# Gradient along rows of an 8192 x 8192 array: from groups of three loads and three stores to strict turns, with a late first store

## The chip, the cores and the metric

One core of one Trainium2 chip. The metric is the device time of one execution in microseconds (us); lower is better. Times are medians of several executions. A ratio is the mean time of one kernel's fast runs over that of the other's fast runs of the same rounds, so it is not quite the ratio of the medians that stand beside it.

Three words are used throughout. A **transfer** is one load or one store of a set, 8.39 MB, that 16 DMA engines carry together; each engine moves 8 rows of 64 KB, one packet per row. A **mark** is the completion write of one engine at the end of its part of a transfer, so a transfer has 16 of them; the **spread** is the time from the first to the last of the 16. A **turn** is the point at which an engine goes from the last packet of a load to the first packet of a store. Packets and marks are records in the trace. They don't name the engine; I put each packet behind the one whose end it follows.

## The reference

```python
def setup_inputs():
    return {"x": np.random.randn(8192, 8192).astype(np.float32)}

def reference(x):
    return np.gradient(x, axis=1)
```

Inside a row, an element of the result is half the difference of its two neighbours; at both ends of a row it is the plain difference of the first or last two elements. 268 MB are read and 268 MB written.

## The kernel before

A set is 256 rows, two per partition (64 KB per partition). There are 32 sets and three slots in SBUF. A set is loaded to a slot, VectorE computes it in place, shifted by 64 elements, and the slot is stored. All loads and stores are issued by SyncE on one queue. `chain` names the steps that an instruction has to wait for, in place of the scheduler's own finding.

```python
    R = 2; NB = 3; SH = 64; W = R * m
    slots = [pool.tile([P, SH + W], f32, ...) for k in range(NB)]
    ...
    def load(i):
        b = slots[i % NB]
        ins = nc.sync.dma_start(out=b[:, SH : SH + W], in_=x_sets[i])
        loads.append(chain(i, ins, *([stores[i - NB]] if i >= NB else [])))

    with tc.manual_schedule():
        for i in range(NB):
            load(i)
        for i in range(nsets):
            ...  # ends: GpSimd takes the 4 edge differences of the set
            for r in range(0, R, nr):        # one pass; two in the last set
                ...  # halved: VectorE, 0.5 * (right - left), whole set
                ...  # placed: VectorE or GpSimd copies the edges in
                ins = nc.sync.dma_start(
                    out=out_sets[i, :, r * m : (r + nr) * m], in_=b[:, r * m : (r + nr) * m]
                )
                stores[i] = chain(i, ins, placed)
                at = [halved]
            if i % NB == NB - 1:
                for k in range(i + 1, min(i + 1 + NB, nsets)):
                    load(k)
```

So the queue holds three loads, three stores, three loads and so on: eleven turns in all.

## Time and profile before

| | before |
|---|---|
| median of 3 runs | 1247.24 us (1247.1 to 1248.14) |
| span of the profiled run | 1245.0 us |
| one queue, share of 16 engines' span | 99.8% |
| VectorE busy | 554.8 us (45%) |
| one transfer, mark to mark | 19.32 us |

The prediction below shows the lines that this table rests on. One more view carries the argument: the table of DMA issues of the page, with the time from issue to landing (us) at the end of each line.

```profile
out_dram<-slot SPq DMA_DIRECT2D x2, 4096.0 KB, 20.2
slot<-in_x_dram SPq DMA_DIRECT2D x32, 58.0
out_dram<-slot SPq DMA_DIRECT2D x31, 40.3
```

A transfer takes 19.3 us, but a load lands 58.0 us after its issue and a store 40.3: two transfers, and one, lie ahead of it in the queue. A queue this full does not run dry before the end of the run, and until then a wait of the issuing engine costs nothing.

### The profile page before, as it was taken

What the parts mean: (1) busy time and instruction counts of PE and PEld (TensorE: products, weight loads), DVE (VectorE), ACT (ScalarE), POOL (GpSimd) and SP (SyncE); (2) the same over time, 40 slices, a digit from 0 to 9 for tenths busy, and PEclk for the clock granted to TensorE, in tenths of its full rate; (3) what the DMA queues carried; (4) which work ended last, traced back from release to release, by engine and by line L of the source; (5) the groups of instructions that cost most, each with busy time, mean ns of one, the idle gap of its engine ahead of it and who ended that gap; (6) DMA issues with size and microseconds to landing.
All of it is one profiled execution on the core that took longest, in us unless ns stands there. A gap on an engine that the chain in (4) does not pass through costs nothing.

```text
span 1245.0 us, 241 instructions
## 1 busy us (share of the span) xinstructions
DVE 554.8 (45%) x54; POOL 8.8 (1%) x48
## 2 busy tenths in 40 slices
DVE  2850483079009603850582079009603840591083
POOL 0000000000000000000000000000000000000000
DMA  9999999999999999999999999999999999999999
GB/s 404 438 436 419 425 438 438 438 438 438 434 427 421 436 438 438 436 438 432 432 419 438 436 438 432 436 434 432 423 436 436 436 438 436 430 427 430 436 411 404
DMA packets 9361, 536.88 MB, mean 431 GB/s; under 512 B 1040, under 2 KB 1040, under 8 KB 1040
## 3 DMA queue, kind: packets, MB, share of 16 engines
q1 hardware_dynamic: 9360, 536.88, 99.8%
q14 instruction: 1, 0.01, 0.0%
HBM read 268.44 MB, written 268.44 MB: 431 GB/s over the span
## 4 chain that ended last, share of the span: by engine, by line
another core or an unknown queue 74%; DVE 18%; DMA 3%; issue 2%; POOL 1%; SPq 0%; POOLq 0%
DVE slot L81 18%; DMA slot<-in_x_dram 3%; POOL ends L70 0%; POOL slot L92 0%; SPq L60 0%; DVE slot L92 0%; POOLq L127 0%
## 5 line engine op out<-in xcount | busy, mean ns | idle before, releaser
L81 DVE CUSTOM_DVE_ANT_0 slot<-slot 128x16382 f32<-128x16382 f32 (+1 forms) x33 | 551.3, 16706 | 667.9 <-POOL ends L70 667.9
L70 POOL TENSOR_TENSOR ends<-slot 128x4 f32<-128x4 f32 x32 | 6.3, 198 | 988.8 <-DMA slot<-in_x_dram 988.8
L92 DVE COPY slot<-ends 128x4 f32<-128x4 f32 (+1 forms) x21 | 3.6, 172 | 0.7
L92 POOL COPY slot<-ends 128x4 f32<-128x4 f32 x12 | 2.3, 190 | 207.9 <-DVE slot L81 207.9
L116 POOL MEMSET const-bfloat16-1.0<- 128x1 bf16 x1 | 0.1, 102 | 0.0
L116 POOL MEMSET const-uint8-127<- 128x1 uint8 x1 | 0.1, 102 | 0.0
L116 POOL MEMSET const-float32-0.0<- 128x1 f32 x1 | 0.1, 99 | 0.2 <-issue 0.2
L116 POOL MEMSET const-float32-1.0<- 128x1 f32 x1 | 0.1, 99 | 0.0
## 6 DMA issues: line engine op xcount, KB each, us to landing
out_dram<-slot SPq DMA_DIRECT2D x2, 4096.0 KB, 20.2
slot<-in_x_dram SPq DMA_DIRECT2D x32, 58.0
out_dram<-slot SPq DMA_DIRECT2D x31, 40.3
```

Source lines behind the costliest of these rows:

```text
L70: ins = nc.gpsimd.tensor_sub(out=ends[:, i, :, :], in0=xin[:, :, 1 : m : m - 2], in1=xin[:, :, 0 : m - 1 : m - 2],)
L81: ins = nc.vector._custom_dve(dve_ops.TENSOR_TENSOR_REDUCE_SUB_MAX, out=b[:, c0:c1], in0=b[:, SH + c0 + 1 : SH + c1 + 1], in1=b[:, SH + c0 ...
L92: ins = placer.tensor_copy(out=res[:, :, 0 : m : m - 1], in_=ends[:, i, r : r + nr, :])
L116: nc = _bacc.Bacc("TRN2", target_bir_lowering=False, num_devices=1)
```

## The change

Two things at once. After the first three loads and two stores, a load follows each store, so the direction changes after every transfer (30 turns; the recorded texts below say 31). And the first store is no longer issued while the loads run: an otherwise useless matmul, which itself waits for the second set's edges, is set ahead of it, so that the third load has run out of the engines before the store arrives. The intent is to start the stores on all 16 engines at once.

```diff
+    unread = psum.tile([1, 128], f32, name="unread", tag="unread")
...
                 placed = chain(i, ins, halved)
-                ins = nc.sync.dma_start(out=out_sets[i, ...], in_=b[...])
-                stores[i] = chain(i, ins, placed)
+                if i == 0:
+                    at = [halved]
+                    first = placed
+                    continue
+                if i == 1:
+                    pause = nc.tensor.matmul(
+                        out=unread[:], lhsT=slots[0][:, 0:1], rhs=slots[0][:, 0:128], start=True, stop=True
+                    )
+                    follow(pause, placed, "towards the end of the third load")
+                    follow(store(0, 0, R, first), pause, "after the third load")
+                store(i, r, nr, placed)
                 at = [halved]
-            if i % NB == NB - 1:
-                for k in range(i + 1, min(i + 1 + NB, nsets)):
-                    load(k)
+            if 1 <= i and i + 2 < nsets:
+                load(i + 2)
```

(`follow` adds one wait between two instructions, and `store` issues the same transfer as before.)

More of the change, by code (lines that the diff above doesn't have):

```diff
@@ L4 @@
 import concourse.tile as tile
-from concourse import bass_utils, dve_ops
+from concourse import bass_utils, dve_ops, mybir
 from concourse._compat import with_exitstack
@@ L41 @@
     ends = pool.tile([P, nsets, R, 2], f32, name="ends", tag="ends")
+    psum = ctx.enter_context(tc.tile_pool(name="psum", bufs=1, space=bass.MemoryType.PSUM))
+    unread = psum.tile([1, 128], f32, name="unread", tag="unread")
     loads, stores = [], [None] * nsets
@@ L56, in chain, with follow @@
         return ins
+    def follow(ins, needed, reason):
+        edge = mybir.DependencyInfo(mybir.DependencyClass.Sync, mybir.DependencyReason.DATA)
+        tc.add_manual_dep(ins.ins, needed.ins.name, edge, reason=reason)
     def load(i):
@@ L61, in load, with store @@
         loads.append(chain(i, ins, *([stores[i - NB]] if i >= NB else [])))
+    def store(i, r, nr, *needed):
+        ins = nc.sync.dma_start(
+            out=out_sets[i, :, r * m : (r + nr) * m], in_=slots[i % NB][:, r * m : (r + nr) * m]
+        )
+        stores[i] = chain(i, ins, *needed)
+        return ins
     with tc.manual_schedule():
@@ L93 @@
                 placed = chain(i, ins, halved)
-                ins = nc.sync.dma_start(
-                    out=out_sets[i, :, r * m : (r + nr) * m], in_=b[:, r * m : (r + nr) * m]
-                )
-                stores[i] = chain(i, ins, placed)
+                if i == 0:
[5 more added lines that the diff above has]
+                        out=unread[:], lhsT=slots[0][:, 0:1], rhs=slots[0][:, 0:128], start=True, stop=True
+                    )
+                    follow(pause, placed, "towards the end of the third load")
+                    follow(store(0, 0, R, first), pause, "after the third load")
+                store(i, r, nr, placed)
                 at = [halved]
-            if i % NB == NB - 1:
-                for k in range(i + 1, min(i + 1 + NB, nsets)):
-                    load(k)
+            if 1 <= i and i + 2 < nsets:
+                load(i + 2)
 _INS = ['x']
```

## The prediction

> **What bounds the kernel now.** I read the page's head and its slices first, then the DMA queue, then the issue-to-landing table, then the waits of the DMA queue and the timeline of the start and of the end; last I took the DMA packet records and the completion marks out of the trace.
>
> ```profile
> span 1245.0 us, 241 instructions
> DVE 554.8 (45%) x54; POOL 8.8 (1%) x48
> ...
> DMA  9999999999999999999999999999999999999999
> GB/s 404 438 436 419 425 438 438 438 438 438 434 427 421 436 438 438 436 438 432 432 419 438 436 438 432 436 434 432 423 436 436 436 438 436 430 427 430 436 411 404
> ...
> q1 hardware_dynamic: 9360, 536.88, 99.8%
> ```
>
> The reader is to see that VectorE is busy 45% of the span, while the DMA row holds a 9 in every one of its 40 slices and the one queue fills 99.8% of sixteen engines' span. The work is 536.88 MB each run, loads and stores together, and no edit of the order changes that. So the kernel is bound by the DMA engines, and only time in which an engine is idle or slower than its best can be won.
>
> How much is that? In the trace one packet is one partition's row of a set, 65,536 bytes; the minimum, the median and the 75th percentile of its duration are all 2.418 us. Sixteen engines each carry 8 such packets per transfer of 8.39 MB. From the completion marks one transfer follows another every 19.32 us nearly all the way through, in groups of loads and in groups of stores alike: 8.39 MB / 19.32 us = 434 GB/s. There are 32 loads and 32 stores (the last store in two halves), so 64 x 19.32 = 1236.5 us of the 1245.0 is transfer at the full rate. The other 8.5 us are:
> - 1.75 us before the first packet and 1.25 us after the last (first packet 1.75, last packet's end 1243.74);
> - about 0.6 us of slow first packets (some 3.0 us against 2.418);
> - about 0.8 us in the last store's two halves (9.72 us each by the mean of the engines, against 9.66) and in marks between transfers, with rounding;
> - 1.1 us at the first store: the third load's mark comes 20.47 us after the second's instead of 19.32, all 16 engines alike, as the last packet of that load takes 3.2 to 3.5 us;
> - the rest, some 3 us, on the slowest engines only, over the middle of the run. The engines' marks of one transfer lie 0.48 us apart at 62 us and 2.57 us apart from 876 us on. I found nearly all of it in one place: the last packet of the third load of a group, just before the engine turns to stores. At ten such turns after the first the last engine to finish lost, by my differences of the marks, about 0.0 to 0.2 us (seven turns) and 0.6 to 0.8 us (three turns, near 525, 642 and 759 us). At the turns from stores to loads I found nothing of note.
>
> The second view is the start and the end:
>
> ```profile
> 0.74 1.33 SPq L60 DMA_DIRECT2D slot<-in_x_dram  x3
> 22.70 0.20 POOL L70 TENSOR_TENSOR ends<-slot 128x4 f32<-128x4 f32 x1 [22.26 <-DMA slot<-in_x_dram]
> 22.93 17.22 DVE L81 CUSTOM_DVE_ANT_0 slot<-slot 128x16382 f32<-128x16382 f32 x1 [22.93 <-POOL ends L70]
> 40.19 0.17 DVE L92 COPY slot<-ends 128x4 f32<-128x4 f32 x1
> 40.39 40.08 SPq L94 DMA_DIRECT2D out_dram<-slot  x3
> ...
> 59.56 0.19 POOL L92 COPY slot<-ends 128x4 f32<-128x4 f32 x1 [17.32 <-DVE slot L81]
> 62.45 0.20 POOL L70 TENSOR_TENSOR ends<-slot 128x4 f32<-128x4 f32 x1 [2.71 <-DMA slot<-in_x_dram]
> ```
>
> Here the first store is issued at 40.39 us, in the middle of the load phase, and stands in the queue until the third load is through, at about 61.7 us. The copy on GpSimd at 59.56 ends at 59.75; it is the event that the new matmul waits for. And the rule of the buffers: the DMA queue's own waits are large but harmless, since a transfer is already under way behind each of them.
>
> ```profile
> SPq L94 <- DVE slot L92: 525.7, 21, 55.9
> SPq L60 <- DMA out_dram<-slot: 373.2, 29, 19.2
> ```
>
> **What the Trainium skill says.** "DMA: Bandwidth & Descriptors", section "Where 436 GB/s comes from", gives 435.2 GB/s for the 16 ports and says that the ports are the bottleneck; the 434 GB/s of a step above agrees, so I allow no gain in the rate itself. Its section "Queues, rings and completion order" says that each engine consumes descriptors in ring order and that nothing is FIFO across engines; the marks that drift from 0.48 to 2.57 us apart agree. "HBM Reference", section "Access", gives about 425 GB/s for a core streaming alone; the trace is a little above. For the added matmul, "TensorE: Matmul & The Clock Gate", section "Single matmul latency", has (219 + N)/1.2 ns cold for bf16, so 0.29 us for N = 128; no matmul is in the trace before, and this one is in float32, so I allow 0.3 to 0.7 us, an estimate.
>
> **The change part by part.**
>
> *Order.* From three loads, three stores to L0 L1 L2 S0 S1 L3 S2 L4 S3 L5 and so on to S29 L31 S30 S31. The same 65 transfers; the packets do not change. Does the new order starve the queue? Count in steps T of 19.32 us from the start of S0: S0 fills 0-1, S1 1-2, L3 2-3, S2 3-4, L4 4-5, S3 5-6, L5 6-7. L3 waits for S0's landing (at 1T plus some 1.5 us) and is wanted at 2T. S3 needs L3 landed (3T + 1.6 us), then 0.23 us of GpSimd, 17.22 us of VectorE and 0.2 us for the ends, so about 4T; it is wanted at 5T. L5 waits for S2, landed just after 4T, and sits behind S3 in the issuing engine, so about 4T + 2 us; it is wanted at 6T. Every later pair repeats this, and each transfer is issued about one T, 19 us, ahead. I expect no starving: **0 us**.
>
> *First store.* It leaves the third load alone. That load should then end 1.0 to 1.1 us earlier, near 60.7 (21.92 + 2 x 19.34 by the marks' mean). But the store now waits for 59.75 (copy) + 0.1 + 0.3 to 0.7 (matmul) + 0.1, so it is issued at about 60.5, and its first packet moves some 1.0 us after issue (the first load: issued 0.74, first packet 1.75), so 61.5; a start from idle costs the first packets up to 0.6 us, as at the start of the kernel. S0 then ends by its mean mark at about 81.0 to 81.6, against 81.07 before: **0 to +0.5 us**.
>
> *What the idle start buys.* All engines start the store together. The kernel's last store, where most engines had run dry, shows a spread of only 0.25 us. If it keeps the engines in step, the 3.2 us that the slowest engine loses between 62 and 1205 us can go: **0 to -3.2 us**.
>
> *The turns.* Load to store turns grow from 11 to 31 or so. If each cost what those ten cost on average, 0.31 us on the slowest engine, that would be 31 x 0.31 = 9.6 us in place of 3.1: **up to +6.5 us**. I don't believe the whole of it: once the engines were 2.57 us apart, more than a packet, the loss all but stopped, and in the new order no store is issued while a load is on its last packet (S3 comes at about 4T, at the end of a store), which before it always was.
>
> *End.* L31 lands, S30 has long been computed, so it follows at once; before, it was issued at 1203.88 and the early engines idled for over a microsecond. The end goes by the late engines, so this is worth **0 to -0.5 us**.
>
> *Sum.* With no loss at the turns: S0's mark at 81.4, + 59 x 19.32 + 2 x 9.72 = 1240.7, + 0.3 to the slowest engine + 1.25 after it = a span of 1242.3; the median time was 2.2 us over the span, so **1244.5 us**. With the losses as before it is about 1247.5, with 0.31 us at each turn about 1253.
>
> **The rivals.** First, *nothing gained*: the drift of the engines comes back at the more numerous turns and saturates near a packet's length, as before; the time is 1247 to 1248. The three costly turns out of eleven, without a visible rule, speak for it; against it, that the group turns coincided with issues. Second, *a turn penalty*: every turn costs, reads and writes of HBM now mix all the time; 1250 to 1254. For it: the loss sits at load to store turns alone. Against: at the turns near 178 and 1106 us there was next to none, and before, too, early engines stored while late ones loaded, with steps still of 19.32. Third, *a wait takes over*, where the compute of a set lies on the path since the loads are no longer a group ahead: each set late by 1 us would cost 30 us. The count of T above speaks against it, as VectorE needs 17.4 us in each 38.6.
>
> **How the range follows.** I give 45% to nearly no loss (1244 to 1245.5), 35% to a loss as before (1246 to 1248.5), 20% to more. The point is 1245.8, the range 1243.7 to 1251. 2% is 25 us: far more than all the idle there is (8.5 us), so faster by over 2% is all but excluded, and slower needs the third rival.
>
> **What would show it.** In the profile after: 99% or more of sixteen engines' span on the one queue and 9s in all slices (no starving); steps of 19.32 us between marks; the third load landing near 61 and the first store issued near 60.5 us; the marks' spread under 0.5 us for long (gain kept) or growing to over 2 us (first rival). GB/s under 430 in the middle slices would speak for the second, a wait of VectorE or of a store that ends with idle engines for the third. A step other than 19.32 us would make the prediction wrong.

## The result, and the profile after

The changed kernel took 1251.85 us in the median (1250.09 to 1253.26, 4 runs) against 1247.42 (1247.1 to 1248.14, 4 runs): 4.4 us more. The ratio is 1.0034, with an interval of 1.0017 to 1.0051. That is within 2%, as forecast, but the time lies outside the range.

The page of the changed kernel, its head, the slices and the queue:

```profile
span 1251.1 us, 246 instructions
...
DMA  9999999999999999999999999999999999999997
GB/s 402 436 436 402 436 436 436 432 436 434 425 436 432 436 436 430 417 427 436 436 434 436 427 434 432 434 436 436 436 436 436 434 430 434 436 427 434 425 436 339
...
q1 hardware_dynamic: 9360, 536.88, 99.5%
```

The engines are nearly as full as before (99.5% against 99.8%), and the DMA row shows no starved stretch before the last slice. Two slices are to be looked at. The fourth (some 94 to 125 us) moved 402 GB/s, where its neighbours have 436. And the last has a 7 and 339 GB/s, where before it had a 9 and 404: in the last 31 us some engines have finished and others have not.

The start of its timeline (start, duration, instruction, and in brackets the idle time before it with what ended it):

```profile
59.48 0.19 POOL L105 COPY slot<-ends 128x4 f32<-128x4 f32 x1 [17.32 <-DVE slot L94]
59.73 0.09 PEld L115 LDWEIGHTS unread<-slot 128*1 128x1 f32 x2 [59.73 <-POOL slot L105]
59.73 0.58 PE L115 MATMUL unread<-slot 128*1 128x128 f32 x2 [59.73 <-POOL slot L105]
60.34 0.83 SPq L70 DMA_DIRECT2D out_dram<-slot  x2
61.31 0.20 POOL L83 TENSOR_TENSOR ends<-slot 128x4 f32<-128x4 f32 x1 [1.63 <-DMA slot<-in_x_dram]
...
121.87 0.20 POOL L83 TENSOR_TENSOR ends<-slot 128x4 f32<-128x4 f32 x1 [60.36 <-DMA slot<-in_x_dram]
```

The pause works as meant: the matmul ends at 60.31, the store is issued at 60.34, and the third load is seen landed at 61.31, where before it was 62.45. The fourth load is seen landed at 121.87. Three transfers of 19.32 us lie between (two stores and the load itself), so 61.31 + 57.96 = 119.27 would do; 2.6 us are gone by then.

The waits of the DMA queue's issuer show that nothing new blocks it. Each column is: total us, times, longest.

```profile
SPq L70 <- DVE slot L105: 665.3, 19, 37.7
SPq L66 <- DMA out_dram<-slot: 71.1, 29, 20.0
SPq L70 <- PE unread L115: 58.3, 1, 58.3
```

The waits for stores to land are now short in total (71.1 us against 373.2 before), since a load is asked for later; the table of issues still has 58.5 us from a load's issue to its landing and 40.2 us for a store, as before. The queue stayed one to two transfers ahead, as the prediction counted.

The marks say where the 6.1 us between the two spans went. (The profiled run of the changed kernel was the slowest of its four, so its trace shows 6.1 us where the medians differ by 4.4.)

| from the marks, us | before | after | difference |
|---|---|---|---|
| first store done, mean of 16 engines | 81.07 | 80.65 | -0.42 |
| the next transfer takes (a store in both) | 19.32 | 20.10 | +0.78 |
| the one after it (a store; now the load of set 3) | 19.32 | 20.44 | +1.12 |
| sixth transfer done, last engine | 120.03 | 121.50 | +1.47 |
| from there to the 63rd transfer, last engine | 1104.34 | 1108.92 | +4.58 |
| spread of the 62nd transfer's marks | 2.57 | 8.02 | |
| last store, to the end | 19.37 | 19.37 | 0 |

The rows that add up are the fourth, the fifth and the last: 1.47 + 4.58 = 6.05 us, the difference between the last packets' ends (1243.74 and 1249.79). There are two losses, then. **One comes once, in the first 125 us, to all engines**: the first store is done 0.4 us sooner, and the next two transfers lose 1.9 us. **The other grows through the run and on the slow engines alone**: 57 transfers at 19.32 us are 1101.24; the last mark fell 3.1 us behind that before and 7.7 us after, while the first mark fell only 0.3 us behind after.

In both traces nearly all of the second loss sits in one packet of eight: the last packet of a load that is followed by a store. Summed over all loads of the changed kernel and averaged over the engines, the excess over 2.418 us of the eight packets of a load is 0.86, 0.00, 0.00, 0.00, 0.00, 0.03, 0.05 and 3.94 us; the first is the start of the kernel, the last the turns (0.9 of the 3.94 belongs to the load of set 3, so to the first loss).

### The profile page after: what moved, and what is told of

It is laid out like the page before. It is cut to its first block, busy times and chain, and to the rows that moved or that the text cites. A ratio compares the mean times of both kernels' runs of the same rounds, so it can differ in the third digit from the quotient of the medians.

```text
span 1251.1 us, 246 instructions
## 1 busy us (share of the span) xinstructions
PE 0.6 (0%) x2; PEld 0.1 (0%) x2; DVE 554.8 (44%) x54; POOL 8.9 (1%) x48
## 3 DMA queue, kind: packets, MB, share of 16 engines
q1 hardware_dynamic: 9360, 536.88, 99.5%
## 4 chain that ended last, share of the span: by engine, by line
another core or an unknown queue 68%; DVE 18%; DMA 8%; issue 3%; POOL 1%; PE 0%; SPq 0%; POOLq 0%
DVE slot L94 18%; DMA slot<-in_x_dram 7%; DMA out_dram<-slot 2%; POOL ends L83 0%; POOL slot L105 0%; PE unread L115 0%; SPq L66 0%; DVE slot L105 0%; POOLq L149 0%
## 6 DMA issues: line engine op xcount, KB each, us to landing
slot<-in_x_dram SPq DMA_DIRECT2D x32, 58.5
out_dram<-slot SPq DMA_DIRECT2D x31, 40.2
```

## The experiments

Two theories to begin with. **A**: the number of turns makes the drift, and the late first store is harmless. **B**: the late first store leaves the engines in a worse state for the whole run, and the turns are harmless. In the first four runs each part of the change was done alone.

**The changed kernel again (e0_after)**, without an edit, as the control.

> The changed kernel again, unaltered, as the control for the three runs beside it. Both theories: 1250 to 1253 us, 3 to 6 us over the kernel before, and a spread of the engines' completion marks that grows to 5 us or more.

Measured: 1251.65 us against 1248.23 on that chip, ratio 1.0036 (1.0023 to 1.005); the spread grew to 5.3 us. The result repeats.

**Strict turns alone (e1_alt_nopause).**

```diff
-                if i == 0: ...            # the deferred first store
-                if i == 1: ...            # the matmul and the two waits
                 store(i, r, nr, placed)
```

> Strict turns, but the first store issued as early as before (no matmul, no pause). Theory A (the number of turns from load to store makes the loss): 1250 to 1253 us as in the changed kernel, with the engines drifting apart by 5 us or more, and the 1.0 us loss at the first store back. Theory B (the late first store sets a bad state for the whole run): 1246 to 1248 us, spread under 3 us.

Measured: 1250.09 us (1248.08 to 1253.06), ratio 1.0016 (1.0003 to 1.0029), 2 us over the kernel before. The 1.0 us at the first store is back; the spread grew to 6.05 us, and the last engine lost 5.8 us from the sixth transfer to the 63rd. The drift belongs to the turns, but the turns alone give half of the loss in time. Its page shows the same end as the changed kernel's (a 7, and 344 GB/s), with no 402 in the fourth slice:

```profile
DMA  9999999999999999999999999999999999999997
GB/s 403 437 437 424 429 424 437 433 433 435 433 431 437 435 426 424 433 433 435 437 437 435 435 426 435 437 433 424 437 437 437 435 435 435 429 435 435 437 437 344
```

**The late first store alone (e2_grp_pause).**

```diff
-            if 1 <= i and i + 2 < nsets:
-                load(i + 2)
+            if i % NB == NB - 1:
+                for k in range(i + 1, min(i + 1 + NB, nsets)):
+                    load(k)
```

> Groups of three as before, but with the late first store. Theory A: 1246 to 1248 us, spread 2 to 3 us at the end, as before. Theory B: 1250 us or more, spread over 5 us. Besides, where the 1.0 us loss of the third load only waits for the first non-idle turn, about 1 us must come back at the next change of direction.

Measured: 1249.75 us, ratio 1.0013 (1.0001 to 1.0026), 1.5 us over the kernel before. Theory A missed here (the spread was 3.75 us in the end), and theory B too; the remark at the end of the expectation came true. By the marks, the third load lost nothing (before: 1.1 us), but the engines then stood idle, and the first store was done at 80.95 us in the mean, hardly sooner than before (81.07). Then the third store, ahead of the first load, lost 0.76 us, and the third load of the next group, at the first turn without a pause, 1.16 us in the mean of the engines. The timeline shows the latter:

```profile
159.93 0.20 POOL L83 TENSOR_TENSOR ends<-slot 128x4 f32<-128x4 f32 x1 [1.64 <-DMA slot<-in_x_dram]
...
180.31 0.20 POOL L83 TENSOR_TENSOR ends<-slot 128x4 f32<-128x4 f32 x1 [20.18 <-DMA slot<-in_x_dram]
```

The two loads are seen landed 20.38 us apart. In the kernel before, the same pair stood 19.36 us apart:

```profile
159.18 0.20 POOL L70 TENSOR_TENSOR ends<-slot 128x4 f32<-128x4 f32 x1 [1.64 <-DMA slot<-in_x_dram]
...
178.54 0.20 POOL L70 TENSOR_TENSOR ends<-slot 128x4 f32<-128x4 f32 x1 [19.16 <-DMA slot<-in_x_dram]
```

**Groups of two (e3_pairs)**, first store early.

```diff
-            if 1 <= i and i + 2 < nsets:
-                load(i + 2)
+            if i % 2 == 1:
+                for k in range(i + 2, min(i + 4, nsets)):
+                    load(k)
```

> Turns of two stores and two loads, first store early: 16 turns from load to store against 11 before and 31 in strict turns. Theory A: between the two, 1247.5 to 1250 us, spread 3 to 6 us. Theory B: as the kernel before, 1247 to 1248 us, since the first store is early.

Measured: 1250.01 us, ratio 1.0016 (1.0003 to 1.0028), spread 3.25 us. Theory B missed. The spread is in theory A's range, but it tells nothing, since three traces of groups of three ended with 2.6 to 3.9 us. What the last engine lost from the sixth transfer to the 63rd tells more: 5.3 us, against 3.1 and 4.2 in the two traces of the kernel before and 5.0 to 8.0 in the four of strict turns. Neither this nor the time tells 16 turns from 30.

So neither theory was whole. The two parts roughly add: 0.13% for the pause and 0.16% for the turns, against 0.36% for both on the same chip. The next run asks what the pause does. **C**: after an idle start of all engines, the next two changes of direction cost again, wherever in the run. **D**: such losses belong to the start of the run.

**The pause in the middle (e4_grp_gap_mid)**: groups of three, first store early, and the same matmul ahead of the store of set 15.

```diff
-                if i == 0:
+                if i == 15:
...
-                if i == 1:
+                if i == 16:
...
-                    follow(store(0, 0, R, first), pause, "after the third load")
+                    follow(store(15, 0, R, first), pause, "after the third load")
```

> Groups of three, first store early as before; the same pause, but ahead of the store of set 15, in the middle of the run. Theory C (an idle start of the engines costs again at the next two changes of direction, wherever it is): the transfer after the pause comes about 1 us late, the last store of that group before the next load loses 0.7 us and the next turn from load to store about 1.1 us on all engines; 1.5 us over the kernel before. Theory D (those losses belong to the start of the run, to addresses or queues used for the first time): no uniform loss of over 0.3 us at the next store to load turn, and 0.3 to 1 us over the kernel before.

Measured: 1250.14 us against 1247.78, ratio 1.0018 (1.0006 to 1.0031). The load of set 17 lost nothing at its turn; the store after the pause was done 2.33 us late in the mean (the early engines had stood idle until the store came, behind the late ones: the spread fell from 2.6 to 0.16 us); the last store of that group lost 0.74 us, and the load of set 20, at the next turn, 1.19 us on all engines. The time, 2.4 us over the kernel before, is more than the 1.5 us that theory C had, and clear of the 0.3 to 1 us of theory D. The timeline:

```profile
642.99 0.58 PE L115 MATMUL unread<-slot 128*1 128x128 f32 x2 [642.99 <-POOL slot L105]
643.61 18.98 SPq L70 DMA_DIRECT2D out_dram<-slot  x3
...
742.92 0.20 POOL L83 TENSOR_TENSOR ends<-slot 128x4 f32<-128x4 f32 x1 [1.64 <-DMA slot<-in_x_dram]
...
763.25 0.20 POOL L83 TENSOR_TENSOR ends<-slot 128x4 f32<-128x4 f32 x1 [20.13 <-DMA slot<-in_x_dram]
```

Again 20.33 us between two loads of a group, at the same distance from the pause as in the run with the pause at the start, but 583 us later. **Theory C holds**: the late first store takes away no cost. It trades the 1.0 to 1.1 us of the first turn for an idle gap of nearly the same size (0.8 to 1.0 us at the start of the run), and the first turn without a gap still pays its 1 us, later; the change from stores to loads ahead of it pays 0.7 to 0.8 us, which it does not without the pause (0.00 to 0.03 us at each such change in the trace of the kernel before). The kernel's own start is an idle start too, and after it the first turn pays 1.0 to 1.1 us, but the change back to loads nothing.

**Stores on ScalarE's queue (e5_two_queues)**, from the version with strict turns and no pause, to ask whether an engine pays for each change of direction: with two queues it can change at every packet.

```diff
-        ins = nc.sync.dma_start(
+        ins = nc.scalar.dma_start(
             out=out_sets[i, :, r * m : (r + nr) * m], in_=slots[i % NB][:, r * m : (r + nr) * m]
```

> Strict turns without the pause, stores issued from ScalarE's queue instead of the one queue, so that an engine may change between load and store packets at every packet. Theory A (each change from load to store costs 0.1 to 0.3 us on an engine): some 250 changes instead of 31, so 1275 us or more. Rival (loads and stores of one engine overlap when they come from two queues, and the turn is hidden): 1243 to 1248 us.

Measured: 1248.91 us in the median, but 1245.89 to 1262.62; the profiled run was the slowest. Theory A in the form "each change costs an engine 0.1 to 0.3 us" is refuted: 1275 us or more it never was. The rival's range, 1243 to 1248 us, holds for two of the six runs, and the median lies above it. In the windows (length, VectorE, GpSimd, clock, DMA share, GB/s) the engines are full until 1180 us and idle for two fifths of the end:

```profile
60.00:600.00 540.00, 228.52 (x22) 3.76 (x19) 1.00 1.00 433
600.00:1180.00 580.00, 256.67 (x24) 3.95 (x20) 1.00 1.00 431
1180.00:1220.00 40.00, 17.40 (x2) 0.20 (x1) 1.00 1.01 428
1220.00:1262.00 42.00, 17.62 (x4) 0.20 (x1) 1.00 0.61 261
```

**Transfers alone (m1, m2)**: kernels that do no compute and give a wrong result, to see whether the drift needs the compute, and which side of the transfer makes it. Four phases with a full stop between; 32 KB rows, so a transfer is 9.68 us. The second kernel has the phases in the order 3, 2, 1, 4.

```python
def turns(count, load, store):
    for i in range(3):
        load(i)
    for i in range(count):
        store(i)
        if 1 <= i and i + 2 < count:
            load(i + 2)

# 1: load x -> slot,        store slot -> out      28 pairs
# 2: load x -> slot,        store slot -> copy     28 pairs
# 3: load copy[0] -> slot,  store slot -> out      28 pairs
# 4: as 1, partitions 0..126, 4 KB each            14 pairs
```

> Transfers alone, no compute, wrong result on purpose; four phases with a full stop between them. 1: HBM to SBUF and SBUF to HBM in strict turns, 32 KB rows. 2: HBM to SBUF and SBUF to SBUF in turns (only the side that is read changes). 3: SBUF to SBUF and SBUF to HBM in turns (only the side that is written changes). 4: 127 partitions of 4 KB rows, loads and stores in turns, expected on one engine alone. Theory E (the loss at a turn from load to store comes from the change of the read side): stretched last packets in 1 and 2, none in 3. Theory F (from the change of the written side): in 1 and 3, none in 2. Where others' traffic makes it, phase 4 shows none; where it is the engine's own, phase 4 shows 0.1 us or more at each turn.

> The same four phases in the order 3, 2, 1, 4, to see whether what a phase shows depends on its place in the run. Both theories: the same losses by phase as in the run before it, within 0.1 us per turn in the mean.

The windows over the four phases of m1:

```profile
20.00:570.00 550.00, 0.13 (x2) 0.00 (x0) 1.00 0.99 426
575.00:1118.00 543.00, 0.07 (x1) 0.00 (x0) 1.00 1.00 430
1125.00:1815.00 690.00, 0.29 (x5) 0.00 (x0) 1.00 0.99 338
1820.00:2370.00 550.00, 0.00 (x0) 0.00 (x0) 1.00 0.06 26
```

Phases 1 and 2 run at the full rate; phase 4 moves 26 GB/s, a sixteenth, and has one mark per transfer: one engine, as meant. From the marks:

| phase | spread at its start, us | at its end, m1 | at its end, m2 |
|---|---|---|---|
| 1: HBM to SBUF, SBUF to HBM | 0.7, 0.5 | 6.84 | 6.64 |
| 2: HBM to SBUF, SBUF to SBUF | 0.8, 0.5 | 0.98 | 1.10 |
| 4: one engine | | every step 19.73 us after the second | the same |

The drift is there without any compute, so VectorE is not needed for it. It is gone where nothing is written to HBM, though the read side changes at each turn just the same; theory E (the read side) is refuted for the drift. The loss of 1.1 us at the first turn, however, is in phase 2 too (10.79 and 10.69 us for that transfer in place of 9.68). And one engine alone pays at no turn. Phase 3, which should have tested the written side alone, tells nothing: its SBUF to SBUF copies took 14.6 to 14.7 us by themselves.

**Fewer engines (m3)**, and phase 3 once more with the SBUF source below its targets.

```diff
-        if which == "D": ...
+        if which in "EFG":
+            rows = {"E": 122, "F": 119, "G": 117}[which]
+            turns(14, lambda i: dma(out=slots[i % 3][:rows], in_=xs[first + i][:rows]),
+                  lambda i: dma(out=os_[first + i][:rows], in_=slots[i % 3][:rows]))
```

> Transfers alone again, wrong result on purpose, 32 KB rows, strict turns, full stop between phases. 1: SBUF to SBUF and SBUF to HBM, with the SBUF source now below its targets in address, as in the phase that ran at full speed. If the change of the written side made the drift: spread growing to 5 us or more with steps of 9.7 us; if it takes HBM reads and HBM writes of different engines side by side: spread under 1.5 us. 2 to 4: HBM to SBUF and SBUF to HBM with 117, 119 and 122 partitions, expected on 13, 7 and 2 engines. If the loss at a turn comes from the other engines' traffic, the loss per turn falls with the number of engines and is under 0.02 us on 2; if not, it is the same for all.

The counts of marks confirm 13, 7 and 2 engines. Over 14 pairs the spread grew from 0.53 to 1.50 us with 13 engines (16 engines, after as many transfers: 5.27 and 4.04 us in m1 and m2), and stayed at 0.11 us with 2, where 28 transfers lost 0.16 us in all. With 7 engines it tells nothing: the rows of 119 partitions ran unevenly from the start, with steps of 20.6 us and more. The SBUF copies were slow again (14.6 to 14.7 us), so the written side alone remains untested.

**The kernel before against itself (e6_before_again), and strict turns a second time (e1b_alt_nopause)**, since the intervals of single parts nearly touch 1.

> The kernel before against itself: how far apart do two equal kernels measure, and is its drift of the engines repeatable? If the differences of 0.13 to 0.18% seen for single parts of the change are real: a ratio within 0.0005 of 1 and an end spread of 2 to 4 us, with under 0.2 us lost at each turn from stores to loads. If they are noise: a ratio as far from 1 as theirs.

> Strict turns without the pause a second time, for a second trace and a second interval: 1.5 to 2.5 us over the kernel before (ratio 1.0012 to 1.002), end spread 5 us or more with eight engines that lose nothing. If the first trace was a chance: spread under 4 us, ratio under 1.0005.

Measured: 1.0002 (0.9989 to 1.0016) for the kernel before against itself, spread 3.9 us, and at most 0.12 us lost at a turn from stores to loads. Strict turns: 1250.69 us, 1.0021 (1.0009 to 1.0034), spread 7.84 us. So a null comparison has an interval of about 0.0014 to each side. The 0.0013 for the pause alone does not clear that, and its own interval leaves 1 out by 0.0001; that the pause costs leans on the marks, where its two losses appear in all four traces with a pause (the changed kernel, e0, e2 and e4), and on e4's 1.0018. In none without a pause does the change from stores to loads lose anything like it. The drift of strict turns is well clear: 5.3 to 8.0 us of spread in four traces, against 2.6 and 3.9 us in groups of three (3.75 with the pause at the start).

**Two queues with the end in order (e7_two_queues_tail28, e8_two_queues_tail30)**, to mend what the run with two queues lost at its end.

```diff
-        ins = nc.scalar.dma_start(
+        queue = nc.scalar if i < 28 else nc.sync     # e8: i < 30
+        ins = queue.dma_start(
```

> Stores of sets 0 to 27 from ScalarE's queue, those of sets 28 to 31 behind the loads on the one queue. In the run with two queues, half of the packets between 60 and 600 us followed a packet of the other direction and nearly all took 2.418 us; the time was lost after 1180 us, where the last load shared the engines with two stores. If the turns between whole transfers are what costs and the tail is mended by this: 1244 to 1246.5 us, faster than both kernels. If mixing by packets has a loss of its own: 1248 us or more, with wide scatter as before.

> The same with only sets 30 and 31 on the one queue: tells how much of the tail must be in order. If the last load is held up by the store of set 30 alone: as the run beside it, 1244 to 1246.5 us. If the store of set 29 holds it up as well: 2 us or more above it, and scatter of several us.

Both missed: 1253.37 us (1247.82 to 1264.69) and 1254.48 us (1248.79 to 1265.27), ratios 1.0052 and 1.0062, with the wide scatter kept. But the packets answer what was open. In the trace of e7, the third fastest of its six runs, 3,841 packets of 64 KB began between 600 and 1180 us, from both queues in nearly equal number until 1080 us, and not one took over 2.45 us. Where a packet's successor on its engine was clear, it came from the other queue in 86 cases of 100. Between 120 and 600 us 19 packets were longer, of 3,180; only the first 60 us after the first store had many (75 of 378). Strict turns on one queue (e1) had 119 between 120 and 600 us, of 3,163, and 27 of 3,840 between 600 and 1180 us. So an engine can go from load to store packets at no cost, and a price per change of direction is no rule. It is not always free with two queues: in the trace of e5, the slowest of its six runs, 176 of 3,811 packets between 600 and 1180 us were longer.

The packets also show where the time with two queues scatters. Counted against 2.415 us for each packet, one engine of e5 was 20.9 us late at 1220 us and the other fifteen 7.5 to 8.3; in e8 one was 7.0 us late and the others 1.9 to 5.6; in e7 they were 3.2 to 9.7 us late, nearly all of it from before 120 us. The last engine sets the end. Why one falls behind is not known.

Here is how the losses lie over the engines, for two turns of the changed kernel. The engines are ordered by the time at which they reach the last packet of the load.

```
set 12   start, us after the first   0.00 0.01 0.03 0.04 0.04 0.06 0.12 0.17   1.25 1.26 1.32 1.72 2.04 2.37 3.65 4.07
         excess over 2.418 us        0    0    0    0    0    0    0    0      0.63 0.50 0.33 0.30 0.44 0.50 1.01 0.70
set 21   start, us after the first   0.00 0.00 0.01 0.01 0.03 0.03 0.14 0.17   4.06 4.10 4.20 4.54 4.69 6.20 6.72 6.76
         excess over 2.418 us        0    0    0    0    0    0    0    0      0.27 0.28 0.22 0.17 0.44 0.25 0.67 0.76
```

Eight engines reach the turn together and lose next to nothing, from about set 12 to the end. The eight behind them make the same turn when the first eight are already storing, and only they lose. So who is late becomes later. But the drift does not grow without end. In the four traces with strict turns the spread reached its last value at 744 us (6.05 us, e1), 883 us (7.84, e1b), 977 us (5.29, e0) and 1018 us (8.02, the changed kernel), and stayed there to within 0.1 us through all later turns; the last five sets lose next to nothing (0.25 us at most on any engine). I have no cause for that.

## Why the prediction was wrong

The bound, the rate, the full queue and the class (within 2%) were right. The sum of small terms was not.

- *What bounds the kernel, and the queue:* right. 19.32 us per transfer in both kernels, 99.5% of the engines' span, no starving, VectorE as before (554.8 us). The rival of a new wait did not come.
- *First store, 0 to +0.5 us:* its parts were right, its sum 0.4 us too dear (measured -0.42). The issue came at 60.34 (said: about 60.5), the matmul took 0.58 us (said: 0.3 to 0.7), the first store's mean mark came at 80.65 (said: 81.0 to 81.6), since its packets began at 61.2 to 61.3 (said: 61.5) and the first ones were not slow (0.06 us over 2.418 at most).
- *What the idle start buys, 0 to -3.2 us:* **this step failed, in its sign.** The idle start did put the engines in step: the first store's spread was 0.16 us. But it bought nothing. The next store lost 0.78 us and the load after it 1.12 us, 1.9 us in all, which the sum did not have (the steps of 20.10 and 20.44 us are the sign of being wrong that the prediction named); I had taken the 1.0 us at the first turn for a cost of issuing early, which a later issue removes. The run with the pause in the middle shows that it comes back after an idle start there as well. Nor did the step hold: with the pause and groups of three the spread was 3.75 us in the end, without it 2.6 and 3.9.
- *The turns, up to +6.5 us, "I don't believe the whole of it":* the mechanism was named and its size wrongly cut. The second rival, a turn penalty with 1250 to 1254 us, came true in its time. The ground for cutting it was that the drift had all but stopped at 2.57 us, "more than a packet". It does not stop there: the spread reached 8.02 us before it stood still. And the trace before was misread: of the seven turns said to lose 0.0 to 0.2 us, the one near 990 us, at 2.6 us of spread, lost 0.37 us, on the last engine and in the mean. The count of turns was 30, not 31. The other ground, that a store used to be issued during the load's last packet, fell as well: in the kernels without compute, and in the new order, no such thing happens, and the drift is there. On the last engine the term was +4.6 us in the trace of the changed kernel (7.7 against 3.1); as a time, strict turns alone cost 1.9 to 2.4 us.
- *End, 0 to -0.5 us:* nothing; the last store took 19.37 us in both, since the last engine had no wait before either.
- *The chances:* a loss at more turns had 20%, a mended drift 45%. The measured 1251.85 is 0.85 us past the upper end of the range.

What is shown: the two parts cost about as much each, and add, within the noise. The pause costs by the two changes of direction after it. The drift came with turns of whole transfers, was next to nothing with one or two engines and where nothing was written to HBM, and needs no compute. What stays open: where in the path of the late engines' last load the time goes; whether the change of the written side alone would do it, since my test of it ran slow; why the drift stops at 5.3 to 8.0 us; and why one engine falls behind with two queues. No version here beats the kernel before beyond the noise.

## What to carry to other kernels

Where 16 DMA engines are full, look at the completion marks of each transfer, not only at the busy share: engines that drift apart add their lag to the end, and a share of 99.5% does not show it before the last slice. Don't split groups of loads and stores on one full queue without need: each change of whole transfers from loading to storing cost the late engines up to 1 us here, and strict turns 1.9 to 2.4 us more than groups of three. And don't expect to save a cost at a change of direction by letting the engines run dry first: it came back, with another one.

## What the Trainium skill lacked or had wrong

- "DMA: Bandwidth & Descriptors" has no cost for a change of direction on a full queue. Here the last packet of a load ahead of a store took 0 to 1.0 us over its 2.418 us on engines that came late to the turn, and the marks of one transfer drifted from 0.16 to 8.02 us apart over a run.
- The same page gives a fixed cost per transfer, but not that an idle start of all engines costs again later: 0.7 to 0.8 us at the next change from stores to loads and 1.1 to 1.2 us at the next from loads to stores, in four traces.
- Its section "Issuing engines are not separate DMA queues" says that only issue time is saved by a second queue. It leaves out that times can then scatter, one engine falling far behind (20.9 us late against 8.3 at most, e5): 1245.89 to 1265.27 us over 18 runs of three kernels, against 1246.23 to 1249.07 us for the kernel before, timed beside them and the other runs.
- Its section "Where 436 GB/s comes from" has SBUF to SBUF transfers bound by the ports at 435 GB/s. Copies of 4.19 MB from three tiles to two ran at that (9.68 us, 433 GB/s), but from a single source tile to three others it took 14.6 to 14.7 us, 286 GB/s, with the source above or below its targets. I have no cause for it.
- "TensorE: Matmul & The Clock Gate", section "Single matmul latency", has a form for bf16 alone. A float32 matmul of N = 128 after a long idle ran as two matmul records and took 0.58 us, twice the 0.29 us of that form.
